# Last weight sums of two units loaded earlier, activation sums beside another product, two accumulator banks taken later

## Chip, cores and metric

The kernel runs on one core of a Trainium2 chip. The metric is the device time of one execution in microseconds; the median of three runs before the change is 613.61 us (612.9 to 615.04). One profiled execution, of 612.21 us, gives the trace.

## The reference

One layer of a hybrid decoder: 512 tokens of width 1024 in float32. A combined input projection feeds a retention group and an indexed sparse attention group; an output projection and a layer norm follow, then the feed-forward part, where the change lies:

```python
gate, up = jnp.split(x @ w_gate_up, 2, axis=-1)      # hidden 2816 = 22 tiles of 128
ffn = (jax.nn.silu(gate) * up) @ w_down              # (512, 2816) @ (2816, 1024)
return layer_norm(DEEPNORM_ALPHA * x + ffn, ln_ffn_gain, ln_ffn_bias)
```

## The kernel before

**Numbers in two halves.** A float32 operand is split into a rounded high part and the rest (`split`, lines 92 to 98): ScalarE casts the high part (L93); the low part is a VectorE subtraction (L98) or, where `None` is passed for the engine, a negating ScalarE copy (L95) and an accumulating GpSimd DMA (L96). `mm3` (lines 100 to 103) makes a product of three matmuls: high x high (L101), low weight (L102), low activation (L103).

**The down projection.** Pairs of hidden tiles are numbered 0 to 10. Pairs 0, 1 and 10 are multiplied plainly (`d_mm`); the other eight form four *units* of two pairs, numbered 1 to 4, and go through a scheme that saves multiplications: seven products q = 1, 5, 6, 2, 4, 7, 3 for each unit, of a sum of activations (`aprep`, tiles named `slot`) with a sum of weights (`w_prep`, tiles `dhp` and `dlp`). The index i runs over `WORDER`, q by q and within it unit by unit; `w_mm(i)` is one product of 12 matmuls of 128x512. "Product i" below is that.

**The weight sums.** `SOURCE` (line 1437 on) names them. `r11`, `r21` and `r22` are plain loads on SP's queue (`q_load`, L87). `sum` is loaded and then added to: by VectorE (`q_sum`, L1435) and twice by accumulating GpSimd loads (`q_add`, L1431), issued as soon as `w_prep` has used the sum before. `t3`, for q = 7, is a load to which another block of the weights is added. For units 3 and 4 VectorE adds `r22` to it (`q_sum`). For units 1 and 2 it lies in four small buffers (`q_load_small`), each loaded on SP and added to by an accumulating GpSimd load (L1429).

**The activation sums.** VectorE forms `ts` in steps s1, s2 and s4 (L1398, L1401, L1404; q = 5, 6 and 3) and `t3s` in s3 (L1408; q = 7).

**The accumulators.** X and Y (two PSUM banks each, tiles `dx`, `dy`) and the four banks `left` (tiles `dl`) collect the products; VectorE takes them into the residual `y` with `take` (L1465) and `add_to` (L1468), and `stat` (L1471) adds a norm statistic. Products 12 to 15 (q = 2) go to `left[0]` and `left[1]`, 16 to 19 (q = 4) to `left[2]` and `left[3]`, 20 to 23 to X. Then four right strips (tiles `dr`) are made: for two of them first `r_step` (18 matmuls each, weights of `conv_w(1, ...)`), then products 24 to 27, which need the X banks free, and the last strip (`ds`, `dc`).

**What sets the order.** The program is written out by hand; each engine follows its own order. Loop body i issues `w_mm(i)` for TensorE and, for the others, the takes and the preparations of later products: `w_prep(i + 4)`, and an `aprep` for four products later. ScalarE's cast for `w_prep(i + 4)` waits until TensorE has finished product i, whose buffer it takes. SP and GpSimd issue DMAs in order, and one that waits for a buffer holds those behind it. GpSimd's accumulating DMAs share one queue.

Of the kernel before, what the change touches and what calls it, by code (L numbers as in the profile page):

```python
# [53 lines left out]
def hybrid_layer_kernel(ctx: ExitStack, tc: tile.TileContext, xT, x, pos, w0, wf, wt, wo,  # L54
# [18 lines left out]
    def tmp(name, dt=F32):  # L73
        return tp.tile([P, 512], dt, tag="t", name=name)
# [11 lines left out]
    def dma(dst, src):  # L86
        nc.sync.dma_start(dst, src)  # L87
# [4 lines left out]
    def split(eng_lo, hi, lo, src):  # L92
        A.copy(hi, src)  # L93
        if eng_lo is None:
            A.activation(lo, src, AF.Copy, scale=-1.0)  # L95
            nc.gpsimd.dma_start(lo.bitcast(F32), src, accum_op=ALU.add)  # L96
        else:
            eng_lo.tensor_tensor(lo, src, hi.bitcast(F32), op=ALU.subtract)  # L98
# [977 lines left out]
    def w_end(n):  # L1076
        g = gp[n]
        V.tensor_tensor(g["h1"], g["h1"], g["t2"][:, :Q], op=ALU.mult)
        V.tensor_tensor(g["h2"], g["h2"], g["t7"][:, :Q], op=ALU.mult)
# [231 lines left out]
    UNITS = [1, 2, 3, 4]  # L1311
# [4 lines left out]
    def wprep(key, pieces, low=V, into=None):  # L1316
        if into:
            both = big.tile([P, 2, 1024], F32R, tag=into, name=f"dw{key}")
            wh, wl = both[:, 0], both[:, 1]
        else:  # L1320
            wh = wp.tile([P, 1024], F32R, tag="wh", bufs=4, name=f"dh{key}")
            wl = wp.tile([P, 1024], F32R, tag="wl", bufs=4, name=f"dl{key}")
        n = 1024 // len(pieces)
        for i, src in enumerate(pieces):
            hi, lo = (t[:, i * n:i * n + n] for t in (wh, wl))
            split(low, hi, lo, src)
        dw[key] = wh, wl

    def flat(t):
        return t.rearrange("p k c -> p (k c)")  # L1330
# [11 lines left out]
    def ten_load(c, tag=None):  # L1342
        t = big.tile([P, 2, S], F32, tag=tag, name=f"d10_{c}") if tag else None
        ten[c] = [t[:, i] if tag else tmp(f"d10_{c}{i}") for i in range(2)]
        for i in range(2):
            dma(ten[c][i], wd[10, :, i, c * S:c * S + S])

    def conv_w(c, k, into=None):
        wprep((c, k), ten[c] if k == 10 else [flat(draw[c][:, 2 * k:2 * k + 2])], V, into)
# [17 lines left out]
    def d_mm(acc, c, m, b, first, last, cs=slice(0, S)):  # L1367
        wh, wl = dw[c, m]
        for k in range(2):
            h, l = dh[m, k]  # L1370
            bs = slice(b * P, b * P + P)
            ws = slice(k * S + cs.start, k * S + cs.stop)
            mm3(acc, h[:, bs], l[:, bs], wh[:, ws], wl[:, ws], first and k == 0, last and k == 1, skip_group_check=True)


    def blk(j, r, k):
        return hu[j].rearrange("p (q k) c -> p q k c", k=2)[:, :, k, r * Q:r * Q + Q]
# [4 lines left out]
    def pq(t):  # L1382
        return t.rearrange("p (q c) -> p q c", q=2)

    def aprep(q, j, src, low):
        i, half = divmod(slot_n[0], 2)
        if half == 0:
            slot_n[1] = big.tile([P, 2, 2, S], F32R, tag=slot_tags[i % len(slot_tags)], name=f"slot{i}")
        slot_n[0] += 1
        t = slot_n[1][:, half]  # L1390
        split(low, pq(t[:, 0]), pq(t[:, 1]), src)
        da[q, j] = t
# [10 lines left out]
    def s4_(j):  # L1403
        V.tensor_tensor(pq(ts[j]), blk(j, 0, 1), pq(ts[j]), op=ALU.add)  # L1404

    def s3_(j):
        t3s[j] = tmp(f"t3s{j}")
        V.tensor_tensor(pq(t3s[j]), blk(j, 0, 0), blk(j, 1, 0), op=ALU.subtract)  # L1408

    def rows_of(j, k, n):  # L1410
        return wd[2 * j:2 * j + 2, :, k, n * S:n * S + S].rearrange("q p c -> p q c")
# [9 lines left out]
    def q_load_small(name, j, k, n):  # L1421
        quad[name, j] = [tmp(f"{name}_{j}{q}") for q in range(2)]
        for q in range(2):
            dma(quad[name, j][q], rows_of(j, k, n)[:, q])

    def q_add(name, j, k, n):
        if isinstance(quad[name, j], list):
            for q in range(2):
                nc.gpsimd.dma_start(quad[name, j][q], rows_of(j, k, n)[:, q], accum_op=ALU.add)  # L1429
        else:  # L1430
            nc.gpsimd.dma_start(quad[name, j], rows_of(j, k, n), accum_op=ALU.add)  # L1431

    def q_sum(name, other, j):
        a, b = quad[name, j], quad[other, j]
        V.tensor_tensor(flat(a), flat(a), flat(b), op=ALU.add)  # L1435
# [4 lines left out]
    def w_prep(i, low=V):  # L1440
        q, j = WORDER[i]
        src = quad[SOURCE[q], j]
        wprep(f"p{q}_{j}", src if isinstance(src, list) else [flat(src)], low)
        if q == 5:
            q_add("sum", j, 1, 1)
        elif q == 6:
            q_add("sum", j, 1, 0)

    def w_mm(i, banks, first, tiles=(0, 1)):
        q, j = WORDER[i]  # L1450
        wh, wl = dw[f"p{q}_{j}"]
        a = da[q, j]
        for n in range(2):
            for t in tiles:
                ss = slice(n * Q + t * P, n * Q + t * P + P)
                ws = slice(n * S, n * S + S)
                mm3(banks[t], a[:, 0, ss], a[:, 1, ss], wh[:, ws], wl[:, ws], first and j == UNITS[0] and n == 0,
                    j == UNITS[-1] and n == 1, skip_group_check=True)

    y = x1  # L1460
    cl, cr = slice(0, S), slice(S, D)
# [5 lines left out]
    def add_to(b, cs, acc, op=ALU.add):  # L1467
        V.tensor_tensor(y[b][:, cs], y[b][:, cs], acc, op=op)  # L1468

    def stat(b, i, cs):  # L1470
        V.bn_stats(stats[b][:, i], y[b][:, cs])  # L1471
# [26 lines left out]
    left = []  # L1498
# [4 lines left out]
    def left_mm(m, b):  # L1503
        d_mm(left[b], 0, m, b, m == 0, False)
# [51 lines left out]
    q_load("sum", 0, 0, 1)  # L1556
    ten_load(0)
    home = (raw_n[0] - 1) % 3
    left_mm(0, 3)
    for b in range(NB):  # L1560
        left_mm(1, b)
# [7 lines left out]
    w_end(NF - 2)  # L1569
    aprep(1, 3, blk(3, 0, 0), V)  # L1570
    w_prep(2)
    q_sum("sum", "r11", 1)
    w_end(NF - 1)
    conv_h(10)
# [20 lines left out]
    for i in range(24):  # L1595
        q, j = WORDER[i]
        u = UNITS[i % 4]
        w_mm(i, home_of[q], q in (1, 5))
        if i == 3:
            l_step(10)  # L1600
        if i == 4:
            for t in range(2):
                take(t, cl, X[t])
        elif i == 8:
            for t in range(2):
                take(t, cr, Y[t], ALU.subtract)
        elif i == 9:
            for t in range(2):
                take(2 + t, cr, Y[t], ALU.subtract)
            for k in UNITS[:2]:  # L1610
                q_load_small("t3", k, 0, 1)
            for k in UNITS[:2]:
                q_add("t3", k, 1, 1)
        elif i == 12:
            for t in range(2):
                add_to(t, cr, X[t], ALU.subtract)
        elif i == 16:
            for b in range(2):
                add_to(b, cl, left[b])
                stat(b, 0, cl)  # L1620
        elif i == 18:
            d_load(1, "X1")
            gf = big.tile([P, 2, D], F32, tag="s8", name="gbf")
            for k, v in enumerate((lfg, lfb)):
                dma(gf[:, k], row(v, D))
        elif i == 20:
            for b in range(2, NB):
                take(b, cl, left[b])
            conv_w(1, 0, "s2")
        elif i == 21:  # L1630
            conv_w(1, 10, "s9")
        elif i == 22:
            conv_w(1, 1, "s10")
        if 1 <= i <= 2:
            q_sum("sum", "r11", UNITS[i + 1])
        if i == 2:
            q_load("r21", 1, 1, 0)
        if i < 4:
            w_prep(i + 4)
            if i < 2:  # L1640
                aprep(5, UNITS[i + 2], pq(ts[UNITS[i + 2]]), V)
            s2_(u)
        elif i < 8:
            aprep(6, u, pq(ts[u]), V)
        elif i < 12:
            aprep(2, u, blk(u, 0, 1), V)
        elif i < 16:
            aprep(4, u, blk(u, 1, 1), None if i % 2 else V)
            s4_(u)
        elif i < 20:  # L1650
            if u in UNITS[2:]:
                q_sum("t3", "r22", u)
            s3_(u)
            aprep(7, u, pq(t3s[u]), None if i % 2 else V)
            if i == 19:
                ten_load(1, "s10")
        else:
            aprep(3, u, pq(ts[u]), None)
        if i >= 4:
            w_prep(i + 4)  # L1660
        if i == 9:
            q_load("t3", 1, 0, 1, at=(home + 1) % 3)
        elif i == 12:
            q_load("r22", 1, 1, 1, at=(home + 2) % 3)
        elif i == 13:
            q_load("r22", 0, 1, 1, at=home)
# [44 lines left out]
    b = last  # L1711
# [90 lines left out]
```

## Time and profile before

| what | value |
|---|---|
| median of three runs | 613.61 us |
| the profiled execution | 612.21 us, its span 610.4 us |
| TensorE clock granted, mean | 0.995 |
| HBM read | 77.14 MB |
| GpSimd's DMA queue (q0) | 39.53 MB |
| SP's DMA queue (q1) | 74.59 MB |
| product 8 begins, first right strip begins | 524.87 us, 574.82 us |

Times in rows of the trace are us from the span's start. A row of a timeline gives start, duration, engine, line, operation, "out<-in" by tile names, shapes, and in brackets the idle time just before with what ended it. Matmuls are pipelined, so one of 0.39 us follows another after 0.23. A row "engine line waited for" of the waits gives total, times and longest. A row of DMA issues gives tile, issuing queue, count, KB of one and the median time from issue to landing.

### The profile page before, as it was taken

How to read it: one execution, taken by the hardware profiler on the slowest of the kernel's cores; microseconds unless marked ns; L12 is line 12 of the kernel's file. 1: busy time of each engine (PE TensorE's matmuls, PEld its weight loads, DVE VectorE, ACT ScalarE, POOL GpSimd, SP SyncE). 2: the span in 40 equal slices, each digit the busy share in tenths (PEclk: the TensorE clock that was granted, in tenths of full speed). 3: DMA queues.
4: the chain of work that ended last, by engine and by line, in shares of the span. 5: the costliest groups of instructions: out<-in, count | busy, mean ns of one | idle time of the engine just before them, and what ended most of it. 6: DMA issues, size and time to landing. Idle time of an engine off the chain costs nothing.

```text
span 610.4 us, 9258 instructions
## 1 busy us (share of the span) xinstructions
PE 600.3 (98%) x3229; PEld 518.3 (85%) x3229; DVE 524.7 (86%) x951; ACT 359.1 (59%) x631; POOL 193.6 (32%) x215
## 2 busy tenths in 40 slices
PE   9999999999999999999999999999999999998996
PEld 7988888888888888889998888888888888886675
DVE  6789877899987897999999889898988889697886
ACT  5454344435653766877657767777776856473801
POOL 0138732421571000241015353444435302340220
PEclk9999999999999999999999999999999999998999
DMA  8887874699973864695448888888888758999422
GB/s 295 240 246 199 218 210 116 166 232 235 195 173 104 293 212 168 156 235 110 139 126 195 198 179 205 169 208 164 205 189 185 189 141 203 264 234 313 94 62 103
DMA packets 51054, 115.49 MB, mean 189 GB/s; under 512 B 9104, under 2 KB 24016, under 8 KB 45504
## 3 DMA queue, kind: packets, MB, share of 16 engines
q0 software_dynamic: 25296, 39.53, 37.3%
q1 hardware_dynamic: 25120, 74.59, 36.3%
q10 hardware_dynamic: 592, 0.79, 0.4%
q8 instruction: 25, 0.41, 0.3%
q14 instruction: 21, 0.17, 0.1%
HBM read 77.14 MB, written 2.10 MB: 130 GB/s over the span
## 4 chain that ended last, share of the span: by engine, by line
PE 81%; issue 5%; DVE 5%; DMA 4%; ACT 3%; POOL 1%; SPq 0%; POOLq 0%; DVEq 0%; ACTq 0%
PE ga L1014 16%; PE gc L1014 8%; PE pf L101 5%; PE pf L102 5%; PE pf L103 5%; PE gb L1014 4%; PE ga L1027 4%; PE pt L102 4%; PE pt L101 4%; PE pt L103 3%; DMA sum<-in_wd_dram 3%; PE acc L245 2%; PE mx L103 2%; PE mx L101 2%; PE mx L102 2%
## 5 line engine op out<-in xcount | busy, mean ns | idle before, releaser
L93 ACT CAST wh<-raw 128x1024 fp32r<-128x1024 f32 x44 | 46.0, 1048 | 31.6 <-issue 11.4
L967 POOL DMA_DIRECT2D t<-t x36 | 30.9, 857 | 79.7 <-DVE t L1067 46.1
L101 PE MATMUL pf<-xh,wh 128*128 128x512 f32 x128 | 50.1, 391 | 0.0
L102 PE MATMUL pf<-xl,wh 128*128 128x512 f32 x128 | 49.9, 390 | 0.0
L103 PE MATMUL pf<-xh,wl 128*128 128x512 f32 x128 | 49.9, 389 | 0.0
L967 POOL DMA_DIRECT2D w<-w x36 | 31.5, 999 | 41.8 <-DVE w L1053 39.7
L98 DVE TENSOR_TENSOR wl<-raw,wh 128x1024 fp32r<-128x1024 f32 x26 | 33.0, 1277 | 12.0 <-ACT wh L93 11.9
L101 PE MATMUL pt<-wh,xh 128*128 128x512 f32 (+1 forms) x96 | 38.5, 401 | 0.0
L102 PE MATMUL pt<-wl,xh 128*128 128x512 f32 (+1 forms) x96 | 37.0, 386 | 0.0
L103 PE MATMUL pt<-wh,xl 128*128 128x512 f32 (+1 forms) x96 | 36.7, 382 | 0.0
L96 POOL DMA_DIRECT2D wl<-raw x18 | 16.6, 923 | 46.6 <-ACT wl L95 45.5
L103 PEld LDWEIGHTS pf<-xh,wl 128*128 128x128 f32 x128 | 24.0, 188 | 5.1
L101 PEld LDWEIGHTS pf<-xh,wh 128*128 128x128 f32 x128 | 24.0, 188 | 4.6
L102 PEld LDWEIGHTS pf<-xl,wh 128*128 128x128 f32 x128 | 24.0, 188 | 4.6
L471 DVE MAX8 m<-score 128x8 f32<-128x256 f32 (+2 forms) x48 | 26.8, 557 | 1.0
L509 POOL TENSOR_TENSOR rs<-ve,half 128x1 f32<-128x1 f32 (+1 forms) x10 | 10.3, 1027 | 53.3 <-DVE ve L508 53.2
L472 DVE MATCH_REPLACE8 score<-m,score 128x256 f32<-128x256 f32 (+2 forms) x48 | 26.0, 542 | 0.0
L982 POOL DMA_DIRECT2D graw<-graw x17 | 24.6, 1449 | 1.3 <-issue 0.9
L454 ACT ACTIVATE lg<-lg 128x256 f32<-128x256 f32 (+2 forms) x24 | 10.9, 474 | 22.7 <-PE lg L453 22.6
L1116 ACT COPY t<-ga 128x512 f32<-128x512 f32 x17 | 10.0, 588 | 23.8 <-PE ga L1014 23.8
L93 ACT CAST dhp<-sum 128x1024 fp32r<-128x1024 f32 x12 | 12.6, 1052 | 16.6 <-DMA sum<-in_wd_dram 8.8
L103 PEld LDWEIGHTS pt<-wh,xl 128*128 128x128 f32 x96 | 18.0, 188 | 3.3
(1191 smaller groups left out, 2004.2 us busy)
## 6 DMA issues: line engine op xcount, KB each, us to landing
graw<-in_wgu_dram SPq DMA_DIRECT2D x22, 1024.0 KB, 5.1
wl<-raw POOLq DMA_DIRECT2D x18, 512.0 KB, 5.2
raw<-in_wo_dram SPq DMA_DIRECT2D x8, 1024.0 KB, 5.6
raw<-in_wf_dram SPq DMA_DIRECT2D x7, 1024.0 KB, 6.5
raw<-in_wt_dram SPq DMA_DIRECT2D x6, 1024.0 KB, 5.8
r<-in_wd_dram SPq DMA_DIRECT2D x12, 512.0 KB, 6.9
w<-w POOLq DMA_DIRECT2D x36, 128.0 KB, 3.1
t<-t POOLq DMA_DIRECT2D x36, 128.0 KB, 4.6
```

Of the source, the lines that this page charges most:

```text
L93: A.copy(hi, src)
L96: nc.gpsimd.dma_start(lo.bitcast(F32), src, accum_op=ALU.add)
L98: eng_lo.tensor_tensor(lo, src, hi.bitcast(F32), op=ALU.subtract)
L101: T.matmul(acc, lhsT=lh, rhs=rh, start=first, stop=False, **kw)
L102: T.matmul(acc, lhsT=lh, rhs=rl, start=False, stop=False, **kw)
L103: T.matmul(acc, lhsT=ll, rhs=rh, start=False, stop=last, **kw)
L471: V.max(m8, a)
L472: V.match_replace(out=a, in_to_replace=m8, in_values=a, imm_value=TAKEN)
L967: nc.gpsimd.dma_start(t[:, :Q], t[:, Q:], accum_op=ALU.add)
L982: nc.gpsimd.dma_start(u[:, :S], u[:, S:], accum_op=ALU.add)
L1014: T.matmul(full[:, :Q] if low else full, lhsT=w[:, i * S + k * P:i * S + k * P + P], rhs=rhs, start=first and not low and k == 0, stop=las ...
L1027: T.matmul(gp[n][acc], lhsT=a[:, i * S + k * P:i * S + k * P + P], rhs=parts[q][:, k, b], start=first and j == 0, stop=j == 11, skip_group ...
```

## The change

It moves instructions and adds or removes none; TensorE's order stays.

- The t3 loads of units 1 and 2 and their accumulating loads leave loop body 9 for the place right after `ten_load(0)` (loads) and after `w_prep(2)` (adds).
- s4 moves from bodies 12 to 15 to bodies 8 to 11, s3 from bodies 16 to 19 to 12 to 15.
- The two VectorE sums of t3 with r22 move from bodies 18 and 19 to 15 and 16, behind `w_prep(i + 4)`.
- `left[0]` and `left[1]` are taken, with their statistic, in body 21 instead of 16.

```diff
     ten_load(0)
     home = (raw_n[0] - 1) % 3
+    for j in UNITS[:2]:
+        q_load_small("t3", j, 0, 1)
     left_mm(0, 3)
...
     w_prep(2)
+    for j in UNITS[:2]:
+        q_add("t3", j, 1, 1)
     q_sum("sum", "r11", 1)
...
         elif i == 9:
             for t in range(2):
                 take(2 + t, cr, Y[t], ALU.subtract)
-            for k in UNITS[:2]:
-                q_load_small("t3", k, 0, 1)
-            for k in UNITS[:2]:
-                q_add("t3", k, 1, 1)
...
-        elif i == 16:
-            for b in range(2):
-                add_to(b, cl, left[b])
-                stat(b, 0, cl)
...
         elif i == 21:
+            for b in range(2):
+                add_to(b, cl, left[b])
+                stat(b, 0, cl)
             conv_w(1, 10, "s9")
...
         elif i < 12:
             aprep(2, u, blk(u, 0, 1), V)
+            s4_(u)
         elif i < 16:
             aprep(4, u, blk(u, 1, 1), None if i % 2 else V)
-            s4_(u)
+            s3_(u)
         elif i < 20:
-            if u in UNITS[2:]:
-                q_sum("t3", "r22", u)
-            s3_(u)
             aprep(7, u, pq(t3s[u]), None if i % 2 else V)
...
         if i >= 4:
             w_prep(i + 4)
+        if 15 <= i <= 16:
+            q_sum("t3", "r22", UNITS[i - 13])
```

On SP's queue, from the d10 loads on, before the change (`t_10` to `t_21` are the small t3 buffers of units 1 and 2, `sum` here is that of units 3 and 4, `t_1` the t3 of units 3 and 4):

```order
L87 DMA d_00_5216<-in_wd_dram 128x512
L87 DMA d_01_5217<-in_wd_dram 128x512
L87 DMA sum_5283<-in_wd_dram 128x2x512 x2
L87 DMA r_0_5287<-in_wd_dram 128x2x512 x2
L87 DMA r_1_5370<-in_wd_dram 128x2x512 x2
L87 DMA t_10_5536<-in_wd_dram 128x512
L87 DMA t_11_5537<-in_wd_dram 128x512
L87 DMA t_20_5540<-in_wd_dram 128x512
L87 DMA t_21_5541<-in_wd_dram 128x512
L87 DMA t_1_5554<-in_wd_dram 128x2x512 x2
```

And after it, from the same loads on:

```order
L87 DMA d_00_5216<-in_wd_dram 128x512
L87 DMA d_01_5217<-in_wd_dram 128x512
L87 DMA t_10_5220<-in_wd_dram 128x512
L87 DMA t_11_5221<-in_wd_dram 128x512
L87 DMA t_20_5224<-in_wd_dram 128x512
L87 DMA t_21_5225<-in_wd_dram 128x512
L87 DMA sum_5295<-in_wd_dram 128x2x512 x2
L87 DMA r_0_5299<-in_wd_dram 128x2x512 x2
L87 DMA r_1_5382<-in_wd_dram 128x2x512 x2
L87 DMA t_1_5556<-in_wd_dram 128x2x512 x2
```

The four small loads have moved past six large ones, and stand ahead of the sum load that waits for its buffer. GpSimd's four adds move likewise, from behind the eight sum adds to ahead of them.

On VectorE, bodies 15 to 17 before (`dlp_4` the low weights of product 19, `dl` the two banks, `t3s` the s3 sums, `dlp_1` and `dlp_2` the low weights of products 20 and 21, L1435 the sum with r22):

```order
L98 TENSOR_TENSOR dlp_4_5679<-sum_5283,dhp_4_5678 128x1024
L1468 TENSOR_TENSOR x_0_1988<-x_0_1988,dl_5163 128x512
L1471 BN_STATS fst_2833<-x_0_1988 128x6
L1468 TENSOR_TENSOR x_0_1988<-x_0_1988,dl_5185 128x512
L1471 BN_STATS fst_2834<-x_0_1988 128x6
L1408 TENSOR_TENSOR t3s_5698<-hu_3183 128x512
L98 TENSOR_TENSOR slot_5700<-t3s_5698,slot_5700 128x512
L98 TENSOR_TENSOR dlp_1_5704<-t_10_5536,dhp_1_5703 128x512
L98 TENSOR_TENSOR dlp_1_5704<-t_11_5537,dhp_1_5703 128x512
L1408 TENSOR_TENSOR t3s_5721<-hu_3597 128x512
```

And after, from the last s3 sum on:

```order
L1408 TENSOR_TENSOR t3s_5684<-hu_4471 128x512
L98 TENSOR_TENSOR dlp_4_5687<-sum_5295,dhp_4_5686 128x1024
L1435 TENSOR_TENSOR t_1_5556<-t_1_5556,r_1_5621 128x1024
L98 TENSOR_TENSOR slot_5703<-t3s_5615,slot_5703 128x512
L98 TENSOR_TENSOR dlp_1_5707<-t_10_5220,dhp_1_5706 128x512
L98 TENSOR_TENSOR dlp_1_5707<-t_11_5221,dhp_1_5706 128x512
L1435 TENSOR_TENSOR t_1_5556<-t_1_5556,r_1_5621 128x1024
L98 TENSOR_TENSOR dlp_2_5729<-t_20_5224,dhp_2_5728 128x512
```

The banks and the s3 sums are gone from here, and the sum with r22 stands ahead of the low parts for product 20.

## The prediction

> **What bounds the kernel now.** I read the page first, then TensorE's waits, then TensorE's timeline in the stage that the change touches, then the queues behind its waits. The page's row of engines:
>
> ```profile
> PE 600.3 (98%) x3229; PEld 518.3 (85%) x3229; DVE 524.7 (86%) x951; ACT 359.1 (59%) x631; POOL 193.6 (32%) x215
> ```
>
> TensorE is the bound, so a change that leaves its instructions alone, as this one does, can give back only TensorE's pauses, and only those in the final stage. Its waits from 480 us on (total, times, longest):
>
> ```profile
> PE dl L103 <- DMA slot<-hu: 2.1, 1, 2.1
> PE dx L103 <- DMA slot<-t3s: 1.5, 2, 1.0
> PE fin L1732 <- ACT diag L1731: 1.3, 1, 1.3
> PE dr L101 <- DVE x L1468: 0.2, 1, 0.2
> ```
>
> Two of them wait for a "slot", an activation sum whose low half is made by a GpSimd DMA. The timeline prices the whole stage:
>
> ```profile
> 513.99 0.39 PE L101 MATMUL dy<-dhp,slot 128*128 128x512 f32 x1
> 524.87 0.39 PE L101 MATMUL dx<-dhp,slot 128*128 128x512 f32 x1
> ...
> 549.88 0.39 PE L102 MATMUL dl<-dlp,slot 128*128 128x512 f32 x1
> 552.39 0.50 PE L103 MATMUL dl<-dhp,slot 128*128 128x512 f32 x1 [2.12 <-DMA slot<-hu]
> ...
> 553.55 0.63 PE L101 MATMUL dl<-dhp,slot 128*128 128x512 f32 x1
> ...
> 556.83 0.39 PE L103 MATMUL dl<-dhp,slot 128*128 128x512 f32 x1
> ...
> 574.82 0.40 PE L101 MATMUL dr<-dw(1, 10)_5822,h 128*128 128x512 f32 x1
> ...
> 583.63 0.50 PE L101 MATMUL dr<-dhp,slot 128*128 128x512 f32 x1 [0.16 <-DVE x L1468]
> ```
>
> Products 4 to 7 (12 matmuls each) run from 513.99 to 524.87: 10.88 / 4 = 2.72 us a product, 0.227 a matmul. Products 8 to 23 should take 16 x 2.72 = 43.5 us and take 574.82 - 524.87 = 49.95: 6.4 lost. The 36 matmuls of the first two right strips should take 8.16 and take 583.63 - 574.82 = 8.81: 0.65 lost. So 7.1 us is all there is to win. The largest piece is the pause in product 17: 552.39 - 549.88 - 0.23 = 2.28 us, and behind it 12 steps in 556.83 - 552.39 = 4.44 us instead of 2.72, another 1.72 at a lower clock (0.86 in the fourth row of the next fence). Together 4.0.
>
> Why is the slot late? DMA by stretch (columns: busy time of PE, PEld, DVE, ACT, POOL, then PE clock, DMA share, GB/s), and single DMAs (times, KB, us to landing):
>
> ```profile
> 496.00:503.00 7.00, 7.00 (x33) 5.79 (x32) 5.63 (x7) 3.87 (x6) 0.00 (x0) 1.00 0.00 1
> 503.00:512.00 9.00, 9.00 (x42) 7.44 (x41) 8.98 (x14) 5.83 (x9) 1.21 (x1) 1.00 0.70 234
> 512.00:530.00 18.00, 18.00 (x81) 14.93 (x80) 14.10 (x18) 7.24 (x9) 6.01 (x6) 1.00 1.06 232
> 551.00:563.00 12.00, 10.61 (x40) 8.62 (x41) 9.33 (x14) 4.01 (x8) 0.88 (x1) 0.86 1.02 332
> ```
> ```profile
> t<-in_wd_dram SPq DMA_DIRECT2D x4, 256.0 KB, 13.1
> t<-in_wd_dram POOLq DMA_DIRECT2D x4, 256.0 KB, 11.7
> slot<-hu POOLq DMA_DIRECT2D x1, 256.0 KB, 11.2
> slot<-hu POOLq DMA_DIRECT2D x1, 256.0 KB, 8.4
> slot<-t3s POOLq DMA_DIRECT2D x1, 256.0 KB, 6.1
> ```
>
> The DMA engines stand still from 496 to 503 and are full from 512 on. GpSimd's own issues:
>
> ```profile
> 533.97 4.05 POOL L1429 DMA_DIRECT2D t<-in_wd_dram  x4
> 541.15 1.21 POOL L96 DMA_DIRECT2D slot<-hu  x1 [3.13 <-ACT slot L95]
> 546.81 1.20 POOL L96 DMA_DIRECT2D slot<-hu  x1 [4.45 <-ACT slot L95]
> ```
>
> The slot of product 17 is issued at 541.15, behind the four t3 adds of 533.97, and lands 11.2 us later, at 552.4, the moment TensorE resumes.
>
> **The change, part by part.**
>
> *The t3 loads and adds go forward.* 1.05 MB of plain load and 1.05 MB of accumulating load leave the full stretch. Price by the page's queues (share is of 16 engines' span, 610.4 us):
>
> ```profile
> q0 software_dynamic: 25296, 39.53, 37.3%
> q1 hardware_dynamic: 25120, 74.59, 36.3%
> ```
>
> 0.363 x 610.4 = 222 us for 74.6 MB gives 3.1 us for the loads; 0.373 x 610.4 = 228 us for 39.5 MB gives 6.0 for the adds. They now follow the d10 loads on SP (487.3) and fill the gap of 496 to 503 and the 0.30 x 9 = 2.7 us free up to 512: 9.1 us into 9.7. What is queued behind them: on SP nothing is held, since the sum load of group one waits for its buffer until 502 anyway; on GpSimd the first sum add comes at 510. The fold of w2 stands ahead of them on GpSimd but shares the engines with them; ScalarE waits for it, and the weights of product 3 hang on that:
>
> ```profile
> 494.70 0.42 ACT L1074 ACTIVATE hu<-w 128x256 f32<-128x256 f32 x1 [4.27 <-DMA w<-w]
> ...
> 503.75 1.23 DVE L98 TENSOR_TENSOR dlp<-r,dhp 128x1024 fp32r<-128x1024 f32 x1
> ```
>
> Product 3 uses these at 513.99 - 5.44 - 2.72 + 0.23 = 506.06, that is 1.1 us after 504.98. The fold already ran beside plain loads, so I take a delay under 1 us: cost 0. Bounds: 0 to 2 (if the fold took 3.1 us longer).
>
> *What the sums gain.* Accumulated sums land late and hold ScalarE, then VectorE:
>
> ```profile
> 526.76 1.05 ACT L93 CAST dhp<-sum 128x1024 fp32r<-128x1024 f32 x1 [5.42 <-DMA sum<-in_wd_dram]
> 530.64 1.05 ACT L93 CAST dhp<-sum 128x1024 fp32r<-128x1024 f32 x1 [2.31 <-DMA sum<-in_wd_dram]
> ...
> 554.90 0.62 ACT L93 CAST slot<-t3s 128x512 fp32r<-128x512 f32 x1 [6.71 <-DVE t3s L1408]
> ```
>
> The plain t3 loads were issued from 516.7 and shared the engines with them. Without those 3.1 us the last sum lands near 527.5, so VectorE starts product 8's work about 3 us earlier than in this view:
>
> ```profile
> 531.72 1.23 DVE L98 TENSOR_TENSOR dlp<-sum,dhp 128x1024 fp32r<-128x1024 f32 x1 [2.05 <-ACT dhp L93]
> ...
> 534.66 1.21 DVE L98 TENSOR_TENSOR dlp<-r,dhp 128x1024 fp32r<-128x1024 f32 x1
> ...
> 543.40 0.68 DVE L98 TENSOR_TENSOR slot<-hu,slot 128x512 fp32r<-128x512 f32 x1
> 544.01 0.68 DVE L1404 TENSOR_TENSOR ts<-hu,ts 128x512 f32<-128x512 f32 x1
> 544.61 1.21 DVE L98 TENSOR_TENSOR dlp<-sum,dhp 128x1024 fp32r<-128x1024 f32 x1
> 545.74 0.68 DVE L1404 TENSOR_TENSOR ts<-hu,ts 128x512 f32<-128x512 f32 x1
> ```
>
> *The sums s4 and s3 move, VectorE's cost.* From start to start a 512-wide step takes 0.60 and a 1024-wide one 1.13. Four s4 steps (2.4 us) now lie in products 8 to 11, ahead of the weights of products 12 to 15; s3 takes their old place. Starting at 530.0: products 8 and 9 need 1.20 + 0.60 + 0.60 + 1.13 = 3.53 each, 10 and 11 2.33 each. Product 12's low weights are ready at 533.5 (needed 524.87 + 4 x 2.72 + 0.23 = 536.0), product 13's at 537.1 (538.7), product 16's at 545.3 (546.9), product 19's at 551.0 (555.0). Nothing waits. Without the 3 us VectorE starts at 532.9: product 12's are ready at 536.4 and product 13's at 539.9: 0.4 + 0.7 = 1.1 us of pause. I take 0 because the rows tie the lateness to the DMA.
>
> *The slots.* Product 17's slot loses the 6.0 us of adds ahead of it: 552.4 - 6.0 = 546.4, or 541.15 + 6.1 = 547.3 by the t3s row; needed at 524.87 + 9 x 2.72 + 0.45 = 549.8. The 2.28 goes. What is late next is product 19's slot: issued at 546.81, needed at 555.2. At 6.1 us it lands at 552.9; at its own 8.4, which it had behind the other slot, at 555.2, just in time; at 11.2 at 558.0, a pause of 2.8. Value 0, since its queue is empty ahead of it. Against it: the X1 and gain loads no longer wait for s3 and start some 7 us earlier, beside it. With s3 done by product 15, ScalarE no longer waits 6.71 us for it: product 21's slot is issued near 552 (product 16 ends at 549.4 and frees a weight buffer, then four half-width casts of 0.5 to 0.6 by the row of 554.90) and lands by 558, needed 560.7; product 23's near 557.5, landing by 563.6, needed 566.1. These 1.5 us of waits go.
>
> *The new wait in VectorE.* The sum with r22 now stands at product 15, ahead of the low parts for product 20. r22 is loaded at 542 and now has the hardware queue nearly alone; landing by 547, it costs nothing before 551.0. If it lands only at 555, VectorE is through the weights of product 20 at 557.9 against 557.7: 0.2 us.
>
> *The two banks at product 21.* Four steps, two 0.60 and two 0.69 wide, 2.6 us, leave product 16 and lie ahead of conv_w(1, 10). VectorE from product 19 on: done with 19 at 559.6; product 20 (two takes, two 1024-wide steps) 563.1; the banks 565.7; conv_w(1, 10) 566.9, needed at 524.87 + 43.5 = 568.4; conv_w(1, 1) near 569.2, needed 571.3; the X banks free at 575, needed 568.4 + 8.16 = 576.6. So the 0.65 goes too, with 1.4 us to spare.
>
> **The sum.** 2.28 + 1.72 (product 17) + 2.4 (the rest of 6.4: products 21, 23 and small ones) + 0.65 = 7.1 us at most; I keep 0.5 for margins of 1.5 us that I can't see to the tenth: -6.6. The profiled execution took 612.2 us (span 610.4); it becomes 605.6. The median of the runs shown, 613.61, lies 1.4 above the profiled one; so 607.0.
>
> **Rivals.**
>
> *VectorE or product 19's slot stays late.* The sums land no earlier (-1.1 us) or the slot comes at 558.0 (-2.8, with 1.7 of lower clock behind it, -4.5). For: both margins are thin. Against: the rows above. Result 608 to 611.5; chance 0.18.
>
> *The lower clock is not the pause's doing.* The row of 553.55 shows a matmul of 0.63 us against 0.39, after a pause of 2.3. If the clock fell for another reason, such as load, the 1.72 stays: 608.7; chance 0.07. The Trainium skill (TensorE: Matmul & The Clock Gate, "What's actually happening") has the half clock come after an idle window of about 3.4 us; this pause is shorter, so that rule would leave the dip unexplained, on this rival's side, though the dip, over by 556.83, is about as long as that window.
>
> *The t3 adds hold the software queue (the slower end).* They take 6.0 us and now stand ahead of the first sum add. If the plain loads beside them pushed them past 510, all sums would land up to x later. TensorE's pause in products 12 and 13 is then 1.1 + x, plus 1.7 of clock. Slower by over 0.3% (1.8 us) from x = 7.1 + 1.8 - 2.8 = 6.1; at the whole 6.0 plus 1.0 of shared time the result is 613.6 + 2.7 = 616.3. Against: the gap of 7 idle us. Chance 0.05.
>
> *Nothing measurable.* All pauses reappear one product later, as VectorE's total work is the same. Against: VectorE has idle time to lose, 2.05 us in the row of 531.72 alone. 613.6; chance 0.08.
>
> **How the numbers follow.** Forecast (605.5 to 608) 0.62, and the rivals 0.18, 0.07, 0.05, 0.08. A measurement of this kernel can tell about 0.3% from no change. Faster: 0.62 + 0.18 + 0.07 = 0.87; same 0.08; slower 0.05. The range goes from 605.0 (7.1 us and the runs' scatter, whose lowest is 0.7 under the median) to 611.5, which leaves out the last two rivals and a tail.
>
> **What would show it.** Right: no wait of TensorE for a slot; clock 1.00 from 550 to 560; matmuls of product 8 to 23 in about 43.5 us; t3 adds landing before 510; ScalarE's wait for the last sum shorter by 2 to 3 us. Wrong: a TensorE wait for a low weight at products 12 and 13 (s4 in the way), a slot that still takes over 8 us, or a VectorE wait at L1435.

## The result and the profile after

| | before | after |
|---|---|---|
| median | 613.3 us (612.9 to 615.04, 4 runs) | 608.06 us (607.6 to 608.67, 4 runs) |
| profiled execution, its span | 612.21 us, 610.4 us | 607.6 us, 605.8 us |

The ratio is 0.991, 95% interval 0.9888 to 0.9931: faster by 0.7 to 1.1%, 5.2 us by the medians (before has four runs here, and three ahead of the prediction). The forecast was 607.0.

TensorE's row of the page after. Its 3229 instructions are the same:

```profile
PE 598.3 (99%) x3229; PEld 518.8 (86%) x3229; DVE 523.1 (86%) x951; ACT 359.1 (59%) x631; POOL 193.4 (32%) x215
```

TensorE's waits from 470 us on, after (total, times, longest):

```profile
PE fin L1731 <- ACT diag L1730: 1.3, 1, 1.3
PE dx L102 <- DVE dlp L98: 0.8, 1, 0.8
PE dx L101 <- ACT dhp L93: 0.5, 1, 0.5
```

No wait for a slot is left, but there are two new ones, for the weights of a product into X. TensorE's timeline says which, and prices the stage. These are the two ends of the stage before, which the prediction does not show:

```profile
497.67 0.39 PE L101 MATMUL dx<-dhp,slot 128*128 128x512 f32 x1
...
598.72 0.28 PE L101 MATMUL ds<-dw(1, 10)_5822,h 128*128 128x256 f32 x1
```

And after:

```profile
498.02 0.39 PE L101 MATMUL dx<-dhp,slot 128*128 128x512 f32 x1
...
505.95 0.39 PE L103 MATMUL dx<-dhp,slot 128*128 128x512 f32 x1
506.85 0.50 PE L101 MATMUL dx<-dhp,slot 128*128 128x512 f32 x1 [0.51 <-ACT dhp L93]
...
508.11 0.50 PE L102 MATMUL dx<-dlp,slot 128*128 128x512 f32 x1 [0.76 <-DVE dlp L98]
508.44 0.40 PE L103 MATMUL dx<-dhp,slot 128*128 128x512 f32 x1
...
527.07 0.39 PE L101 MATMUL dx<-dhp,slot 128*128 128x512 f32 x1
...
540.66 0.39 PE L101 MATMUL dl<-dhp,slot 128*128 128x512 f32 x1
541.11 0.50 PE L102 MATMUL dl<-dlp,slot 128*128 128x512 f32 x1
...
570.99 0.39 PE L101 MATMUL dr<-dw(1, 10)_5822,h 128*128 128x512 f32 x1
...
579.14 0.39 PE L101 MATMUL dr<-dhp,slot 128*128 128x512 f32 x1
...
594.11 0.28 PE L101 MATMUL ds<-dw(1, 10)_5822,h 128*128 128x256 f32 x1
```

The rows at 498.02 and 527.07 are the first matmuls of products 0 and 8, those at 570.99 and 579.14 the first right strip and product 24, that of 594.11 the last strip. Their differences:

| stretch | before | after |
|---|---|---|
| start to product 0 | 497.67 | 498.02 |
| products 0 to 7 and the steps of pair 10 between them | 27.20 | 29.05 |
| products 8 to 23 (43.5 without a pause) | 49.95 | 43.92 |
| two right strips | 8.81 | 8.15 |
| products 24 to 27 | 15.09 | 14.97 |

So 6.03 + 0.66 + 0.12 = 6.81 us came back, 1.85 was newly lost in product 3 and 0.35 lies ahead of the stage: 4.61, the difference of the two profiled executions. Matmuls follow one another after 0.23, so the loss in product 3 is 506.85 - 505.95 - 0.23 = 0.67 at its first matmul, about 1.03 at its second and 0.10 at its third, 1.80 in all.

Busy time by stretch after (columns as in the prediction). The gap of 496 to 503 is largely filled (0.70 where 0.00 stood), the clock stays at 1.00 between 551 and 563, and VectorE has no idle time left there:

```profile
496.00:503.00 7.00, 7.00 (x32) 5.80 (x31) 6.64 (x10) 1.75 (x4) 3.53 (x4) 1.00 0.70 176
503.00:512.00 9.00, 7.74 (x33) 5.86 (x32) 8.14 (x11) 7.71 (x12) 0.00 (x0) 1.00 1.00 250
...
551.00:563.00 12.00, 12.00 (x54) 9.93 (x53) 12.00 (x16) 8.62 (x14) 1.74 (x2) 1.00 1.03 302
```

GpSimd's issues after, then how long single DMAs took to land (the fold of w2, which is an accumulating DMA for the last hidden tile; a t3 add; the slots of products 17 and 19):

```profile
499.03 3.53 POOL L1429 DMA_DIRECT2D t<-in_wd_dram  x4 [7.16 <-DMA t<-in_wd_dram]
513.09 1.20 POOL L1431 DMA_DIRECT2D sum<-in_wd_dram  x1 [10.53 <-DVE dlp L98]
...
543.27 1.19 POOL L96 DMA_DIRECT2D slot<-hu  x1 [7.79 <-ACT slot L95]
549.05 1.20 POOL L96 DMA_DIRECT2D slot<-hu  x1 [4.59 <-ACT slot L95]
```
```profile
w<-w POOLq DMA_DIRECT2D x1, 128.0 KB, 7.4
...
t<-in_wd_dram POOLq DMA_DIRECT2D x4, 256.0 KB, 5.6
...
slot<-hu POOLq DMA_DIRECT2D x1, 256.0 KB, 4.0
...
slot<-hu POOLq DMA_DIRECT2D x1, 256.0 KB, 4.6
```

The slot of product 17 now lands at 543.27 + 4.0 = 547.3, where TensorE needs it at 527.07 + 9 x 2.72 + 0.45 + 0.32 = 552.3 (0.32 is the pause at product 13). It is issued 2.1 us later than before, 543.27 against 541.15, and takes 4.0 us where it took 11.2.

Where the pause in product 3 comes from, in ScalarE's and VectorE's timelines after:

```profile
495.64 0.42 ACT L1074 ACTIVATE hu<-w 128x256 f32<-128x256 f32 x1 [4.86 <-DMA w<-w]
...
531.67 1.06 ACT L93 CAST dhp<-sum 128x1024 fp32r<-128x1024 f32 x1 [0.97 <-DMA sum<-in_wd_dram]
```
```profile
496.09 0.69 DVE L1398 TENSOR_TENSOR ts<-hu 128x512 f32<-128x512 f32 x1 [3.03 <-ACT hu L1074]
...
506.82 1.23 DVE L98 TENSOR_TENSOR dlp<-r,dhp 128x1024 fp32r<-128x1024 f32 x1
```

The step of L1398 is s1 of unit 2. It waits 3.03 us for a ScalarE step of the last hidden tile, whose input it does not read. The reading, which s1_later tests: the small t3 tiles, now taken early, have used the free small buffers, and the tile of s1 got the one that the last fold of w2 uses until 496. VectorE's later steps stand behind it, and the low weights of product 3 are made from 506.82 on instead of 503.75.

### The profile page after: what moved, and what is told of

Same layout as the page of the kernel before. It is cut to its first block, busy times and chain, and to the rows that moved or that the text cites. A ratio compares the mean times of both kernels' runs of the same rounds, so it can differ in the third digit from the quotient of the medians.

```text
span 605.8 us, 9258 instructions
## 1 busy us (share of the span) xinstructions
PE 598.3 (99%) x3229; PEld 518.8 (86%) x3229; DVE 523.1 (86%) x951; ACT 359.1 (59%) x631; POOL 193.4 (32%) x215
## 4 chain that ended last, share of the span: by engine, by line
PE 90%; issue 4%; DMA 3%; DVE 1%; POOL 1%; ACT 0%; SPq 0%; POOLq 0%; ACTq 0%; DVEq 0%
PE ga L1014 17%; PE gc L1014 8%; PE pf L102 5%; PE pf L101 5%; PE pf L103 5%; PE gb L1014 4%; PE ga L1027 4%; PE pt L102 4%; PE pt L101 4%; PE pt L103 3%; PE acc L245 3%; PE mx L103 2%; PE mx L101 2%; PE mx L102 2%; PE gc L1027 2%
```

## Experiments

Twelve kernels, in three groups: the new pause, the parts of the change alone or left out, and what stands behind the first pause. "Stage" is the time from product 0's to the last strip's first matmul in the profiled execution: 598.72 - 497.67 = 101.05 us before, 594.11 - 498.02 = 96.09 after. It leaves out that product 0 began at 497.5 to 499.8 us in these executions, a scatter that the medians carry.

### s1_later: the new pause

```diff
     s1_(1)
-    s1_(2)
...
     w_end(NF - 1)
+    s1_(2)
```

> The changed kernel with s1 of unit 2 moved on VectorE from ahead of product 1's weights to behind w_end(NF - 1). Theory one (buffer): TensorE's new pause in product 3 (1.8 us) comes from s1 of unit 2 being given the buffer of the last w2 fold, so that VectorE stands 3.0 us and everything behind it is late. Then the pause goes, VectorE's L1398 waits for nothing, product 3's low weights are ready about 2.1 us earlier, and the time falls by 1.6 to 1.9 us to about 606.3. Theory two (contention): the fold itself lands later because the t3 loads share the DMA engines (7.4 us to landing instead of 6.8), and the pause follows from that; then moving s1 leaves over 1 us of the pause and the time within 0.7 us of 608.06.

606.38 us, ratio 0.9885 (0.9865 to 0.9904), 1.7 under the median after. VectorE's wait at L1398 and the pause in product 3 are gone (products 0 to 7: 27.20), while the fold still lands as late (ScalarE's wait for it 4.8 us). So the buffer that s1 was given did it, and not a later landing of the fold. Stage 94.26.

### early_t3_only: the t3 loads and adds alone

To the kernel before, whose body 9 loses the same four lines:

```diff
+    for j in UNITS[:2]:
+        q_load_small("t3", j, 0, 1)
     left_mm(0, 3)
...
     w_prep(2)
+    for j in UNITS[:2]:
+        q_add("t3", j, 1, 1)
```

> The kernel before with nothing but the t3 loads and adds of units 1 and 2 moved forward; s3, s4, the r22 sums and the two banks stay. Theory one (the adds stood ahead of the slot): product 17's pause and its low clock go (4.0 us), the waits of products 21 and 23 for the t3s slots stay (about 2 us), and the new pause of product 3 (1.8 us) comes in full: about 610.8 us. Rival (VectorE's order does the work): product 17 still waits over 1.5 us, the time is 613 to 615.

613.88 us, ratio 1.0003 (0.999 to 1.0016): nothing, where I had expected 610.8. The pause of product 17 is gone all the same. It has come back at product 21, longer:

```profile
562.97 0.39 PE L102 MATMUL dx<-dlp,slot 128*128 128x512 f32 x1
567.22 0.71 PE L103 MATMUL dx<-dhp,slot 128*128 128x512 f32 x1 [3.86 <-DMA slot<-t3s]
```

That is 567.22 - 562.97 - 0.23 = 4.02 us, with lower clock behind it. Stage 101.28, of which 1.3 is the pause in product 3 (1.8 after the change).

### order_only and adds_late: the t3 step back where it was

order_only is after with the loads and adds of t3 in body 9 again; adds_late moves only the adds back. The edit of order_only, then that of adds_late, to the kernel after:

```diff
-    for j in UNITS[:2]:
-        q_load_small("t3", j, 0, 1)
...
-    for j in UNITS[:2]:
-        q_add("t3", j, 1, 1)
...
+            for k in UNITS[:2]:
+                q_load_small("t3", k, 0, 1)
+            for k in UNITS[:2]:
+                q_add("t3", k, 1, 1)
```
```diff
-    for j in UNITS[:2]:
-        q_add("t3", j, 1, 1)
...
+            for k in UNITS[:2]:
+                q_add("t3", k, 1, 1)
```

> The changed kernel with the t3 loads and adds back in loop body 9: only the moves on VectorE are left. Theory one: no pause in product 3; product 17 waits for its slot as before (2.3 us and the lower clock behind it); products 12 and 13 pause by about 1.1 us because s4 now stands ahead of their weights and the sums land as late as before; the waits for the t3s slots are gone: 611 to 612.5 us. Rival (VectorE's order does the work): product 17's wait is gone or under 1 us, the time is 607 to 609.

607.42 us, ratio 0.9902 (0.9884 to 0.9919): not 611 to 612.5. With the software queue loaded as before, the slot of product 17 (issued 542.39, landing 9.2 us later, 551.6) does not stop TensorE, since TensorE comes later: it loses 0.55, 0.74 and 0.79 us at products 11, 12 and 13, waiting for low weights. Its waits:

```profile
PE dl L102 <- DVE dlp L98: 1.0, 2, 0.5
PE dx L102 <- DVE dlp L98: 0.3, 1, 0.3
```

VectorE's timeline shows that only two of the three can be due to s4:

```profile
532.36 1.23 DVE L98 TENSOR_TENSOR dlp<-sum,dhp 128x1024 fp32r<-128x1024 f32 x1 [1.99 <-ACT dhp L93]
...
535.30 0.68 DVE L1404 TENSOR_TENSOR ts<-hu,ts 128x512 f32<-128x512 f32 x1
```

The low weights of product 11 (532.36) stand ahead of the first s4 step (535.30); they are late because the last sum landed late, its cast starting 6.47 us after product 8 instead of 5.77. Those of products 12 and 13 stand behind s4. Stage 96.12. So the pause at product 17 and its low clock, the 4 us that the prediction gave to the t3 step, go without that step, for 2.1 us of new pauses ahead of it. The slot landed only 0.4 us before its use at 552.0.

> The changed kernel with the plain t3 loads early and the accumulating t3 loads back in loop body 9. Theory one (order in the software queue): product 17's slot is again behind the four adds and lands 9 to 11 us after its issue; its pause comes back in good part (1 to 2.3 us, with the lower clock if it is long): 609.5 to 612 us. Rival (the sheer DMA load): with the plain loads gone from the full stretch the slot lands in 7 us or less and nothing pauses there: within 0.7 us of 608.06. Product 3's pause of 1.8 us stays in both, since the buffers are the same.

608.22 us, ratio 0.9915 (0.9893 to 0.9936). A pause in product 3 is there (1.2 us), so the early loads suffice for one; product 13 loses 0.78. The slot of product 17 takes 8.4 us, between the two expectations, and stops nothing.

### s3_only: the s3 step alone

To the kernel before:

```diff
             aprep(4, u, blk(u, 1, 1), None if i % 2 else V)
             s4_(u)
+            s3_(u)
         elif i < 20:
...
-            s3_(u)
```

> The kernel before with one move alone: the s3 sums go from bodies 16 to 19 to bodies 12 to 15, behind s4, which stays there; t3 loads, r22 sums and banks stay as before. New theory (two limits in a row: product 17's slot behind the DMA queue, product 21's slot behind s3 on VectorE; each alone costs what the other would): product 17 still pauses 2 us or more with the low clock behind it, the waits of products 21 and 23 are gone: 611 to 612 us. Rival (s3 is the whole gain of the moves on VectorE): 607 to 609 us.

610.39 us, ratio 0.9934 (0.9915 to 0.9953), a little under the 611 to 612 expected: the largest part that was tried alone, 3.7 us. Waits of TensorE:

```profile
PE dl L103 <- DMA slot<-hu: 1.0, 1, 1.0
PE dx L102 <- DVE dlp L98: 0.7, 1, 0.7
PE dr L102 <- DVE dw(1, 10)_5822 L98: 0.6, 1, 0.6
```

The waits at products 21 and 23 are gone. TensorE resumes in product 17 as late as before (27.57 us after product 8 began, 27.52 before), but its pause there is down to 1.17 us, since it came later: it lost 0.90 at product 11, among others. With no pause over 1.2 us there is no lower clock. In the right strips, which take 9.75, are new pauses.

### s3_and_t3 and s3_t3_r22: adding the parts up

s3_and_t3 is s3_only with the t3 loads and adds early and s1 of unit 2 later; s3_t3_r22 adds the move of the r22 sums. The edit of s3_and_t3 to s3_only (body 9 loses the four t3 lines), then that of s3_t3_r22 to s3_and_t3:

```diff
+    for j in UNITS[:2]:
+        q_load_small("t3", j, 0, 1)
...
-    s1_(2)
...
+    for j in UNITS[:2]:
+        q_add("t3", j, 1, 1)
...
     w_end(NF - 1)
+    s1_(2)
```
```diff
-            if u in UNITS[2:]:
-                q_sum("t3", "r22", u)
             aprep(7, u, pq(t3s[u]), None if i % 2 else V)
...
             w_prep(i + 4)
+        if 15 <= i <= 16:
+            q_sum("t3", "r22", UNITS[i - 13])
```

> The move of s3 alone together with the early t3 loads and adds, and s1 of unit 2 behind w_end(NF - 1); s4, the r22 sums and the banks stay as before. New theory (two limits in a row): with both taken away no product from 8 to 23 pauses over 0.5 us and the time is 606 to 607.5 us, although each alone gave nothing or little. Rival (the moves of s4 and the banks are needed): 609 us or more, with pauses at products 20 to 23.

607.86 us, ratio 0.9899 (0.9878 to 0.9919), above the 606 to 607.5 expected. As expected, no product from 8 to 23 pauses over 0.5 us; they take 43.74 us, the least of all runs. But the right strips take 10.16:

```profile
PE dr L102 <- DVE dw(1, 10)_5822 L98: 1.1, 1, 1.1
```

ScalarE waits 6.1 us for an r22 sum there, so the conversion of the strip's weights comes late.

> s3_and_t3 (before the change, with s3 in bodies 12 to 15, the t3 loads and adds early, and s1 of unit two later) with the two sums of t3 with r22 in bodies 15 and 16 behind the low weights, as after the change. Theory (in s3_and_t3 ScalarE waits 6.1 us for these sums and conv_w(1, 10) comes 1.2 us late for it): ScalarE's wait for L1435 falls under 3 us, the first right strip's pause under 0.3 us, time 606.0 to 606.8, equal to s1_later. Rival (the right strip is late because VectorE is full with the takes of bodies 19 to 21): the pause of 1.2 us stays, time 607.5 to 608.2.

606.46 us, ratio 0.9881 (0.9861 to 0.9902), equal to s1_later. ScalarE's wait for L1435 and the strips' pause are gone (8.16). One pause of 0.95 is left in the profiled execution, which was the slowest of the five (608.17 us), at product 19, whose slot took 9.6 us to land:

```profile
558.30 0.50 PE L103 MATMUL dl<-dhp,slot 128*128 128x512 f32 x1 [0.79 <-DMA slot<-hu]
```

Stage 94.92.

### banks_back: the banks taken in body 16 again

To s1_later:

```diff
+        elif i == 16:
+            for b in range(2):
+                add_to(b, cl, left[b])
+                stat(b, 0, cl)
...
         elif i == 21:
-            for b in range(2):
-                add_to(b, cl, left[b])
-                stat(b, 0, cl)
             conv_w(1, 10, "s9")
```

> The changed kernel with s1 of unit 2 later, and the two banks taken in body 16 as before. If the move of the banks carries part of the gain, VectorE's 2.6 us in body 16 make the weights of product 20 late and TensorE pauses there by 0.3 to 1 us: 606.7 to 607.4 us. If VectorE has that much slack at this place: within 0.3 us of 606.38.

606.07 us, ratio 0.9863 (0.9844 to 0.9882), strips 8.16: beside the other moves, the banks' place is worth nothing by the time (stage 94.77 against 94.26 in one execution each, with small pauses at products 13 and 21).

### s4_behind and order_s4_behind: the s4 sums behind the weights

The same edit, to s1_later and to order_only:

```diff
             aprep(2, u, blk(u, 0, 1), V)
-            s4_(u)
...
             w_prep(i + 4)
+        if 8 <= i < 12:
+            s4_(u)
```

> The changed kernel with s1 of unit 2 later, and s4 of bodies 8 to 11 behind the weights of products 12 to 15 instead of ahead of them. The pause left at product 13 (0.24 us) goes, if s4 ahead of the weights makes it: about 606.1 us, a difference that the timing hardly tells from 606.38; the trace tells whether the pause is there.

606.24 us, ratio 0.9862 (0.9841 to 0.9882). The pause at product 13 stays as it was in s1_later (0.24 against 0.23), so s4 ahead of the weights is not what makes it; one of 0.63 appears at product 16. Nothing won.

> order_only (the t3 loads and adds back in body 9, all else as after the change) with the four s4 sums behind the low weights of bodies 8 to 11 instead of ahead of them. Theory (in order_only 2.1 us of pauses at products 11 to 13, which the s4 sums cause, bring product 17 later and so hide the lateness of its slot): the pauses at 11 to 13 fall under 0.8 us in sum, product 17 comes 1 us or more earlier, its slot is issued near 542 and lands 8 us or more later, and TensorE waits for it 0.5 to 2 us, with lower clock behind it if it is over 2; time 606.8 to 609.5, that is no gain on order_only's 607.4 beyond 0.6. Rival (the t3 adds' place is worth nothing once VectorE's order is changed): no wait at product 17, time 605.5 to 606.5.

608.48 us, ratio 0.9909 (0.9892 to 0.9925). A mixed answer. Products 11 to 13 lose about 1.0 us instead of 2.1, but product 16 now loses 0.63, so TensorE reached the third matmul of product 17 at 553.3, just after its slot landed (issued 543.08, 10.1 us later, 553.2). The wait that I expected did not show, the gain of the rival did not either. Stage 95.66 against 95.04 in s4_behind.

### t3_no_clash and t3_and_banks: what stands behind the first pause

t3_no_clash is early_t3_only without the buffer clash. t3_and_banks takes, besides, the two banks in body 21. The edits, to early_t3_only and to t3_no_clash:

```diff
-    s1_(2)
...
     w_end(NF - 1)
+    s1_(2)
```
```diff
-        elif i == 16:
-            for b in range(2):
-                add_to(b, cl, left[b])
-                stat(b, 0, cl)
...
         elif i == 21:
+            for b in range(2):
+                add_to(b, cl, left[b])
+                stat(b, 0, cl)
```

> Before the change, with the t3 loads and adds of units 1 and 2 early and s1 of unit two issued after the last weight step (so that it takes no buffer of the last w2 fold); the four sums, the banks and the r22 sums stand as before. Theory (early t3 frees product 17, but s3 for product 21 then stands too late on VectorE, so nothing is won): no pause in product 3, none at product 17, the pause at product 21 stays 3.5 us or more with lower clock behind it; products 8 to 23 take 49 to 51 us; time 612.0 to 614.0. Rival (the buffer clash in product 3 is what ate the gain of the early t3 in early_t3_only): pause at 21 under 2 us, time 607 to 610.

612.6 us, ratio 0.9978 (0.9964 to 0.9993). Product 3 is whole, product 17 does not wait, and the pause at product 21 is 4.43 us:

```profile
561.34 0.39 PE L102 MATMUL dx<-dlp,slot 128*128 128x512 f32 x1
566.00 0.80 PE L103 MATMUL dx<-dhp,slot 128*128 128x512 f32 x1 [4.27 <-DMA slot<-t3s]
566.59 0.63 PE L101 MATMUL dx<-dhp,slot 128*128 128x512 f32 x1
```

So it is not the clash that eats the gain. VectorE's and GpSimd's timelines of the same run say what does:

```profile
550.81 0.68 DVE L1468 TENSOR_TENSOR x<-x,dl 128x512 f32<-128x512 f32 x1
...
552.85 0.69 DVE L1471 BATCH_NORM_STATS2 fst<-x 128x6 f32<-128x512 f32 x1
553.46 0.67 DVE L1408 TENSOR_TENSOR t3s<-hu 128x512 f32<-128x512 f32 x1
...
556.63 0.69 DVE L1408 TENSOR_TENSOR t3s<-hu 128x512 f32<-128x512 f32 x1
```
```profile
558.81 0.88 POOL L96 DMA_DIRECT2D slot<-t3s  x1 [10.22 <-PE dl L103]
```

The two banks (four steps, 550.81 to 553.46) stand ahead of the s3 sums; the second s3 sum, at 556.63, is the one that product 21's slot is made from.

> t3_no_clash with the two banks taken in body 21 instead of 16, nothing else. In early_t3_only these four steps (552.57 to 555.21, 2.64 us) stand right ahead of the first s3 sum on VectorE, ScalarE waits 5.84 us for that sum, and the slot of product 21 follows from the second. Theory (VectorE's order is the second limit): the slot of product 21 is issued 1.5 to 2.7 us earlier against product 16's start, TensorE's wait for it falls to 0.8 to 2.5 us with no or a shorter time at lower clock, products 8 to 23 take 45 to 47.5 us; the right strips may lose up to 1.5; time 608.5 to 610.5. Rival (the queue of the slots or the load of the DMA engines is what makes product 21 late): the wait stays above 3 us, time 612 to 614.

611.51 us, ratio 0.9964 (0.9947 to 0.998). The slot of product 21 is issued 2.0 us earlier against product 8 (557.07 - 526.05 = 31.02; 558.81 - 525.75 = 33.06), TensorE's pause there falls to 1.28, and products 8 to 23 take 46.32 instead of 50.61, though product 17 now pauses by 0.75 (its slot took 9.4 us). But the right strips take 12.42 instead of 8.16:

```profile
562.52 0.39 PE L102 MATMUL dx<-dlp,slot 128*128 128x512 f32 x1
564.03 0.50 PE L103 MATMUL dx<-dhp,slot 128*128 128x512 f32 x1 [1.12 <-DMA slot<-t3s]
...
572.37 0.39 PE L101 MATMUL dr<-dw(1, 10)_5822,h 128*128 128x512 f32 x1
575.09 0.50 PE L102 MATMUL dr<-dw(1, 10)_5822,h 128*128 128x512 f32 x1 [2.34 <-DVE dw(1, 10)_5822 L98]
...
576.37 0.46 PE L101 MATMUL dr<-dw(1, 0)_5795,h 128*128 128x512 f32 x1
576.62 0.63 PE L102 MATMUL dr<-dw(1, 0)_5795,h 128*128 128x512 f32 x1
...
580.01 0.40 PE L101 MATMUL dr<-dw(1, 1)_5846,h 128*128 128x512 f32 x1
```

4.29 us won and 4.26 lost; the stage is 100.90 against 100.93. This execution (613.21 us) was among the slowest of eleven; by the medians some 1.1 us of the gain stays (611.51 against 612.6). The expected 608.5 to 610.5, with at most 1.5 us lost in the strips, was missed: my theory had the right limit at product 21, and had not seen how near the one behind it was.

## Why the prediction was right, and where it was not

*The bound.* Right: TensorE's work is the same, and what came back (6.81 us) is its pauses in the final stage, of the 7.1 named.

*The number.* In part luck. Between the two profiled executions the forecast missed by 2.0 us (605.6 against 607.6), nearly all of it the new pause in product 3. By the medians it missed by 1.1, because the execution profiled before lay 1.1 us under its median and the one after 0.5 under.

*"The delay under 1 us: cost 0" for the early t3 step.* This term was wrong: 1.80 us. That is inside the stated bounds of 0 to 2, but these were for another cause, a slower fold. The fold of w2 did land only 0.6 us later (7.4 against 6.8 us, as ScalarE's wait of 4.86 against 4.27), the delay that was argued. What the step did not ask is which buffer each later small tile gets when four tiles are taken early. s1_later shows the whole 1.8 us by moving one line.

*The sums land about 3 us earlier.* Mis-sized. The last cast of a sum starts 531.67 - 527.07 = 4.60 us after product 8 instead of 5.77: 1.2 us. Over all traces it is 3.6 to 5.1 us with the t3 loads and adds early, and 5.8 to 6.9 with both in body 9, so the direction is sound. By the prediction's working s4 then costs something. The trace has 0.32 us at product 13, but before the change 0.19 stood there already, and s4_behind does not remove it. Without any gain (order_only) products 12 and 13 lose 1.5, where the prediction had 1.1; with s4 behind the weights (order_s4_behind) they still lose 0.9, so s4 accounts for only a part.

*Product 17's slot.* The pause with its low clock is gone, and the slot lands at 547.3, where it was put; that is luck, since it was issued 2.1 us later and took 2.1 us less than assumed (4.0 for 6.1). Nor is the short landing shown to be the adds' doing alone: with the adds early and s4 in its old place it took 7.0 to 9.4 us (table below). What failed is the next sentence, "What is late next is product 19's slot", and with it the 4.0 us credited to the t3 step. Product 19's slot landed at 549.05 + 4.6 = 553.7, 4.1 us before its use; in other versions it did stop TensorE, for 0.95 us in s3_t3_r22 and 0.3 in early_t3_only. What is late next is product 21's slot, behind the s3 sums on VectorE: with the t3 step alone it stops TensorE for 4.0 to 4.4 us. Even after the whole change it has little to spare: it was issued at 554.64, about where the prediction had it against product 8, but took 8.3 us instead of 6 and landed 0.3 us before its use. The reverse holds too: with VectorE's moves alone TensorE comes to product 17 later and the slot is in time. Two limits lie behind one another, and a third, the weights of the right strips, behind them.

*"These 1.5 us of waits go" for s3.* They go, but alone s3 is worth more than they are, 3.7 us: products 8 to 23 take 46.29 instead of 49.95, because the low clock behind product 17 goes too, where the pause is now split between products 11 and 17. That product 11 waited (for a sum that landed late, 6.93 us after product 8) is nothing that s3 did, so in that trace part of the gain is not its own. Together with the t3 step it is what lets that step pay. Beside VectorE's moves the t3 step without the clash is worth 96.12 - 94.26 = 1.9 us of stage (order_only to s1_later) or 95.66 - 95.04 = 0.6 (with s4 behind the weights); by the medians it is 1.0 and 2.2, so its size is not settled.

*The sums with r22.* The move was priced as a possible cost and found free, which holds. That it has a worth was not seen: s3_and_t3 and s3_t3_r22 differ by 1.4 us for it by the medians, with intervals that overlap, and their right strips by 2.0.

*The banks.* The strips did lose their 0.65 of pauses, but not by the banks: banks_back has them at 8.16 too. Their four steps cost VectorE 2.64 us wherever they stand; ahead of s3 they hold product 21, ahead of conv_w(1, 10) they can hold the strips.

*The rivals.* That the lower clock is not the pause's doing has fallen: without the pause there is no low clock (the row of 551 to 563), and pauses elsewhere bring it (below). The t3 adds held no queue: issued by 502.6 and landing in 5.6 us by the median, they were done about 5 us before the first sum add at 513.09, which waits for VectorE. The rival that all pauses come back later was wrong for the whole change, and is exactly what its first part does alone.

*What stays open.* How much of the spread in the slots' landing (below) is the queue's and how much the transfers' beside it, and with it how much of the gain at product 17 belongs to s4's move. Of the versions tried, s1_later, banks_back, s4_behind and s3_t3_r22 (606.07 to 606.46) can't be told apart; each is 1.6 to 2.0 us under the kernel after by medians. The intervals of s1_later (0.9865 to 0.9904) and s3_t3_r22 (0.9861 to 0.9902) still meet that of the kernel after (0.9888 to 0.9931), those of the other two (up to 0.9882) do not.

## What to carry to other kernels

Removing a pause of the bounding engine gains no more than the slack of the next thing that this engine would wait for; so before a fix is priced, walk forward from the pause with the engine moved up by its length, and ask of every later input, and not only of those of the same kind, when it is ready. When a load is moved forward, ask also which buffer each tile allocated after it now gets, and who still uses that buffer. Where executions scatter ahead of the stage in question, compare the stage from one fixed instruction to another.

## What the runs showed of the hardware

The clock fell to about half after some pauses in full work and not after others. After 2.28 us (before), 2.49 (t3_and_banks), 4.02 and 4.43 us, matmuls took 0.63 us instead of 0.39 for a while: in t3_and_banks from 576.4, 1.3 us after the work resumed, to 580.0. After 1.03, 1.17 and 1.28 us (after, s3_only, and t3_and_banks at 564.03) they did not. So every pause of this stage from 2.28 us up was followed by the low clock and none up to 1.28; no pause in between was seen. The Trainium skill (TensorE: Matmul & The Clock Gate, "What's actually happening") puts the half clock behind an idle window of about 3.4 us that runs freely; the pauses of 2.28 and 2.49 us were shorter, and the measurement decides, while the 3.6 us of low clock in t3_and_banks is about as long as that window.

The accumulating GpSimd DMA of 256 KB that makes the slot of product 17 took 4.0 to 11.2 us from issue to landing in the fourteen traces, and the time goes with what was issued around it. The third column says how long after it the first of four plain loads of 512 KB (r22, on SP's queue) was issued:

| t3 adds, s4 | traces | r22 loads after the slot's issue | slot, issue to landing |
|---|---|---|---|
| early, bodies 8 to 11 | after, s1_later, banks_back, s4_behind | 2.4 to 2.6 us | 4.0 to 4.3 us |
| early, bodies 12 to 15 | early_t3_only, t3_no_clash, t3_and_banks, s3_and_t3, s3_t3_r22 | -0.9 to 0.3 us | 7.0 to 9.4 us |
| body 9, either | before, s3_only, adds_late, order_only, order_s4_behind | 1.2 to 3.0 us | 8.4 to 11.2 us |

With the adds out of its queue, the slot landed fast in every trace where the r22 loads came behind it, and slowly in every trace where they came at about the same time. No run moved these loads alone, so that they are the cause is not shown. The landing time of such a transfer in one trace is no price for it in another version of the kernel.
